# A quarter of the weights' low parts on another engine in one layer's first pass

## The chip, the core and the metric

The kernel runs on one core of a Trainium2 chip. Its engines work side by side and meet at semaphores: TensorE (PE) multiplies matrices, VectorE (DVE) and ScalarE (ACT) work element by element, GpSimd (POOL) does a few small things here, and SyncE's queue (SP) issues the loads. The metric is the device time of one execution in microseconds.

## What is computed

A trunk of two layers over 256 positions of width 2048. The first layer mixes with pooling and gated linear attention, the second with RWKV-7 and dilated attention; each has a feed-forward of width 8192 and a gate behind it. The second layer's mixer, cut to what matters:

```python
z = h @ w_in                                   # 2048 -> 6432
hc, hd = z[..., :RWKV_IN], z[..., RWKV_IN:]
c_out = rwkv7_time_mix(hc, mu, ...)            # r, k, v and three low-rank inputs from hc
q, k, v = jnp.split(hd, 3, axis=-1)            # dilated attention, with rotary q and k
...
mix = jnp.concatenate([c_out, d_out], axis=-1)
return mix @ w_out
```

All of it is in float32.

## The kernel before

Every large product is made of float32r products: a weight block of 128x1024 numbers is loaded as `raw`, ACT rounds it to `hi` (L257), and DVE makes the low part `lo = raw - hi` (L258). The activations are split likewise into `th` halves. PE adds three products, high by high, high by low and low by high; in `aform_run`, which serves the K, R and V projections, these are the matmuls of L353, L354 and L355, eight contraction tiles to a weight block, and L355 is the one that reads `lo`. In `bform_run` (L328 to L330) L329 reads it.

A weight block goes through `load` (SP's queue, five `raw` buffers), `parts_of` (ACT, then DVE; four buffers each of `hi` and `lo`) and PE. `take` keeps up to two blocks split and up to four in all ahead of the matmuls. In the RWKV layer `self.early` is 30, by which these instructions are given precedence over others.

A planner (Tile) sets the order of DVE's, ACT's, POOL's and SP's instructions by the order in which the program issues them and their precedence, and each engine then works its queue in order. PE's order is written by hand: in `odd`, a `Drive` runs streams (the projections) and chains (small work with due times, in microseconds of its own clock) and emits PE's instructions in that sequence.

In `odd` a first `drive.run` handles the low-rank inputs (six loads of L0, one of them made ahead by `lead`), then 24 blocks of K, R and V in this order, two loads each. The low-rank loads and the first two K loads are queued as four, one, two, one. Beside them run the chains `rate` (with POOL's copy into `decay`, L955), `norm` (squares `sq`, split into `sqh` and `sql`, and the matmul of L968), `operands` and `inner` (the matmuls of L1028). This run ends when the last of the eight `inner` is done, while V's projections still go on. Then new pools are opened, and POOL clears their tiles: EB, LB and CD (L1100), Z and XS (L1103, L1104). A second `drive.run` lets the rest of V, the attention's values and its rotary keys and queries stream on, and beside them `invert()`: transposes into `G` (L1142), 31 steps of a product and a sum on DVE (L821, L1149), and transposes back (L1151, L1153), whose result the matmuls of L1188 read. It ends when `invert()` and `begin()` are through. POOL has no other work of size in the layer.

Of the kernel before, what the change touches and what calls it, by code (L numbers as in the profile page):

```python
# [9 lines left out]
F32 = mybir.dt.float32  # L10
# [3 lines left out]
ALU = mybir.AluOpType  # L14
# [86 lines left out]
class Drive:  # L101
# [4 lines left out]
    def __init__(self):  # L106
        self.t, self.chains, self.streams = 0.0, [], []
# [44 lines left out]
class Trunk:  # L152
    def __init__(self, ctx, tc, a, out, parts=None, taps=None):
        self.tc, self.nc, self.a, self.out = tc, tc.nc, a, out
        self.parts, self.taps = parts, taps or {}
        pool = lambda name, bufs, **kw: ctx.enter_context(tc.tile_pool(name=name, bufs=bufs, **kw))
        self.const = pool("const", 1)
        self.keep = pool("keep", 1)
        self.wr, self.wh, self.wl = pool("wr", 5), pool("wh", 4), pool("wl", 4)
        self.tp = pool("tp", 18)  # L160
        self.acc = pool("acc", 3, space=PSUM)
        self.mp = pool("mp", 5, space=PSUM)
        self.small = pool("small", 3)

        self.gap = pool("gap", 1)
        self.junk = pool("junk", 2)
        self.rbp = pool("rbp", 1)
        nc = self.nc

        self.vec = self.const.tile([P, NVEC + 24], F32, name="vec")[:, :NVEC]  # L170
        nc.sync.dma_start(out=self.vec, in_=a["vec"])
        self.ident = self.const.tile([P, P], F32, name="ident")
        nc.sync.dma_start(out=self.ident, in_=self.cst("ident"))
        self.one = self.const.tile([P, P], F32, name="one")
        nc.vector.memset(self.one, 1.0)

        ps = self.mp.tile([P, 512], F32, name="mp")
        for n in range(10):
            nc.tensor.matmul(ps[:, :P], self.one, self.one, start=True, stop=True)
        self.eps = self.const.tile([P, 2], F32, name="eps")  # L180
        nc.vector.memset(self.gap.tile([P, 16], F32, name="gap"), 0.0)
        nc.vector.memset(self.eps[:, 0:1], EPS)
        nc.vector.memset(self.eps[:, 1:2], LN_EPS)
        self.x = [[self.keep.tile([P, 512], F32, name=f"x{tt}{c}") for c in range(4)] for tt in range(2)]
        self.ls = None
        self.early = 0
        self.pending, self.fetched, self.loaded, self.led = [], [], [], 0
        self.load_x(0)
        if parts and parts[0] != "even":
            for c in range(1, 4):  # L190
                self.load_x(c)
# [59 lines left out]
    def parts_of(self, raw, w, n):  # L251

        nc = self.nc
        hi = self.wh.tile([P, 1024], F32R, name="hi")
        lo = self.wl.tile([P, 1024], F32R, name="lo")
        with self.tc.high_priority(offset=self.early):
            nc.scalar.copy(out=hi[:, :w], in_=raw[:, :w])  # L257
            nc.vector.tensor_tensor(out=lo[:, :w], in0=raw[:, :w], in1=hi[:, :w].bitcast(F32), op=ALU.subtract)  # L258
        return (hi[:, :w].rearrange("p (a n) -> p a n", n=n), lo[:, :w].rearrange("p (a n) -> p a n", n=n))

    def split(self, ps, hi, lo, scale=None):
# [531 lines left out]
    def odd(self):  # L793
# [4 lines left out]
        nc, tc, a = self.nc, self.tc, self.a  # L798
        R0, K0, V0, L0, Q0 = 0, 1024, 2048, 3072, 3360
        w = a["od_w_in"]  # L800
# [22 lines left out]
        with ExitStack() as st:  # L823
# [76 lines left out]
            with ExitStack() as sa:  # L900
# [158 lines left out]
                def first():  # L1059
# [9 lines left out]
                    drive.chain(low(), W["low"], after_low)  # L1069
                    yield from kg  # L1070

                ll, kl = self.b_loads(w, L0, 288), self.a_loads(w, K0)
                self.queue(ll[:4] + kl[:1] + ll[4:] + kl[1:])
                drive.stream(first(), lambda: drive.chain(norm(0), W["key"], normed))
# [321 lines left out]
            def begin():  # L1396
                for g in begun:
                    for step in g:
                        if step[1] < 0:
                            break  # L1400
                        yield step
# [5 lines left out]
            drive.chain(invert(), W["inv0"], lambda: inverted.append(0))  # L1407
            drive.chain(begin(), W["begin"], lambda: inverted.append(1))
            drive.run(lambda: len(inverted) == 2)
            sb.__exit__(None, None, None)  # L1410

            drive.chain(gate_weights())
# [116 lines left out]
```

## Time and profile before

| | us |
|---|---|
| median of 3 runs | 2496.87 (2495.05 to 2496.88) |
| the profiled execution | 2495.14 |
| its span, first to last instruction | 2493.3 |
| busy PE / DVE / ACT / POOL | 2471.3 / 1544.2 / 1317.4 / 14.5 |
| `lo` on DVE (L258), 838 instructions | 1007.3, mean 1.21 each |

Busy times are sums over the span; an engine's idle time costs only where PE waits for it. The first pass of RWKV lies at about 1190 to 1392 us of the span. In a timeline a row is: start, duration, engine, line, operation, output and inputs, shape, count, and in brackets the idle time ahead of it with what ended it.

### The profile page before, as it was taken

Reading aid. Unit: us, or ns where it says so; the run is one execution under the profiler, and the core shown is the slowest. Engines: PE = TensorE matmul, PEld = TensorE weight load, DVE = VectorE, ACT = ScalarE, POOL = GpSimd, SP = SyncE. Lnnn points to the kernel's source line nnn. Section 1 sums busy time; section 2 is a strip of 40 time slices with the busy share of each in tenths; the row PEclk is TensorE's granted clock in tenths of the full one; section 3 lists DMA queues with packets and bytes.
Section 4 is the critical chain, followed back from the end, with each engine's and each line's share of the span. In section 5 each row is a group of like instructions: output and inputs, shape, how many; then the busy total and the mean of one; then the engine's idle time right before and its main releaser. Section 6 shows DMA issues by size and latency. Waiting matters only on the chain.

```text
span 2493.3 us, 36360 instructions
## 1 busy us (share of the span) xinstructions
PE 2471.3 (99%) x14202; PEld 2155.8 (86%) x14202; DVE 1544.2 (62%) x2121; ACT 1317.4 (53%) x1968; POOL 14.5 (1%) x32
## 2 busy tenths in 40 slices
PE   9999999999999999999999999999999999999999
PEld 8888988888888888888999999878888888888888
DVE  6665656555555555576689887656555555555574
ACT  7555546554444444465784565556454444444463
POOL 0000000000000000000000000000000000000000
PEclk9999999999999999999999999999999999999999
DMA  7635765666666666556768754656666666666654
GB/s 247 184 110 151 227 199 168 190 192 190 194 191 189 193 192 187 196 180 201 199 213 241 218 147 135 228 178 182 191 192 189 193 192 190 192 191 190 194 186 143
DMA packets 533084, 471.55 MB, mean 189 GB/s; under 512 B 40352, under 2 KB 417952, under 8 KB 532400
## 3 DMA queue, kind: packets, MB, share of 16 engines
q1 hardware_dynamic: 532912, 469.23, 62.2%
q8 instruction: 111, 1.82, 0.3%
q14 instruction: 61, 0.50, 0.1%
HBM read 456.57 MB, written 12.58 MB: 188 GB/s over the span
## 4 chain that ended last, share of the span: by engine, by line
PE 94%; DVE 3%; ACT 2%; issue 1%; DMA 1%; SPq 0%; DVEq 0%; ACTq 0%
PE acc L373 21%; PE acc L328 18%; PE acc L329 18%; PE acc L330 18%; PE acc L376 11%; PE acc L355 1%; PE acc L354 1%; PE acc L353 1%; DVE lo L258 1%; PE mp L721 1%; ACT hi L257 1%; PE mp L402 1%; DVE x L450 0%; PE mp L672 0%; PE mp L1028 0%
## 5 line engine op out<-in xcount | busy, mean ns | idle before, releaser
L258 DVE TENSOR_TENSOR lo<-raw,hi 128x1024 fp32r<-128x1024 f32 (+2 forms) x838 | 1007.3, 1210 | 768.7 <-ACT hi L257 523.0
L257 ACT CAST hi<-raw 128x1024 fp32r<-128x1024 f32 (+2 forms) x838 | 874.3, 1044 | 935.9 <-PE acc L330 588.2
L373 PE MATMUL acc<-th,hi 128*128 128x512 f32 x2240 | 538.1, 391 | 0.0
L373 PEld LDWEIGHTS acc<-th,hi 128*128 128x128 f32 x2240 | 412.0, 188 | 80.0
L328 PE MATMUL acc<-hi,th 128*128 128x512 f32 (+4 forms) x1248 | 439.1, 353 | 2.5 <-ACT th L264 1.2
L329 PE MATMUL acc<-lo,th 128*128 128x512 f32 (+4 forms) x1248 | 430.2, 345 | 0.4 <-DVE lo L258 0.4
L330 PE MATMUL acc<-hi,th 128*128 128x512 f32 (+4 forms) x1248 | 430.3, 346 | 0.0
L329 PE MATMUL acc<-lo,hh 128*128 128x512 f32 x1024 | 398.7, 389 | 0.0
L330 PE MATMUL acc<-hi,hl 128*128 128x512 f32 x1024 | 398.4, 389 | 0.0
L328 PE MATMUL acc<-hi,hh 128*128 128x512 f32 x1024 | 397.6, 391 | 0.0
L376 PEld LDWEIGHTS acc<-th,lo 128*128 128x128 f32 x2240 | 287.1, 191 | 10.8
L376 PE MATMUL acc<-th,lo 128*128 128x256 f32 x2240 | 290.9, 283 | 0.0
L328 PEld LDWEIGHTS acc<-hi,th 128*128 128x128 f32 x1248 | 235.6, 189 | 31.6 <-DVE y L1454 2.0
L330 PEld LDWEIGHTS acc<-hi,th 128*128 128x128 f32 x1248 | 235.5, 189 | 25.6 <-issue 0.3
L329 PEld LDWEIGHTS acc<-lo,th 128*128 128x128 f32 x1248 | 235.9, 189 | 24.7 <-DVE lo L258 0.7
L328 PEld LDWEIGHTS acc<-hi,hh 128*128 128x128 f32 x1024 | 192.2, 188 | 43.1 <-DVE h L382 3.5
L330 PEld LDWEIGHTS acc<-hi,hl 128*128 128x128 f32 x1024 | 192.2, 188 | 40.0
L329 PEld LDWEIGHTS acc<-lo,hh 128*128 128x128 f32 x1024 | 192.3, 188 | 38.6
L355 PE MATMUL acc<-th,lo 128*128 128x256 f32 x384 | 108.9, 284 | 2.7 <-DVE lo L258 2.7
L353 PE MATMUL acc<-th,hi 128*128 128x256 f32 x384 | 109.3, 285 | 0.0
L354 PE MATMUL acc<-th,hi 128*128 128x256 f32 x384 | 108.6, 283 | 0.0
L486 DVE TENSOR_TENSOR hl<-h,hh 128x512 fp32r<-128x512 f32 x64 | 44.2, 691 | 82.6 <-ACT hh L485 82.6
(319 smaller groups left out, 1754.6 us busy)
## 6 DMA issues: line engine op xcount, KB each, us to landing
raw<-in_ffn_up_dram SPq DMA_DIRECT2D x256, 512.0 KB, 4.0
raw<-in_ffn_down_dram SPq DMA_DIRECT2D x256, 512.0 KB, 4.2
raw<-in_od_w_in_dram SPq DMA_DIRECT2D x96, 512.0 KB, 4.3
raw<-in_ple_gate_dram SPq DMA_DIRECT2D x64, 512.0 KB, 4.4
raw<-in_ev_w_in_dram SPq DMA_DIRECT2D x56, 512.0 KB, 4.3
raw<-in_ev_w_out_dram SPq DMA_DIRECT2D x32, 512.0 KB, 4.3
raw<-in_od_w_out_dram SPq DMA_DIRECT2D x32, 512.0 KB, 4.1
raw<-in_ev_w_in_dram SPq DMA_DIRECT2D x24, 384.0 KB, 3.5
```

What stands on the lines that cost most here:

```text
L257: nc.scalar.copy(out=hi[:, :w], in_=raw[:, :w])
L258: nc.vector.tensor_tensor(out=lo[:, :w], in0=raw[:, :w], in1=hi[:, :w].bitcast(F32), op=ALU.subtract)
L328: nc.tensor.matmul(ps[tt][:, :n], xh[:, t], wh[:, j], start=first and not (joint and tt), stop=False)
L329: nc.tensor.matmul(ps[tt][:, :n], xh[:, t], wl[:, j], start=False, stop=False)
L330: nc.tensor.matmul(ps[tt][:, :n], xl[:, t], wh[:, j], start=False, stop=last and not (joint and not tt))
L353: nc.tensor.matmul(ps, wh[:, j], xh, start=k + j == 0, stop=False)
L354: nc.tensor.matmul(ps, wh[:, j], xl, start=False, stop=False)
L355: nc.tensor.matmul(ps, wl[:, j], xh, start=False, stop=k + j == kts - 1)
L373: nc.tensor.matmul(ps[e], ws[e][0][:, j], xT[k + j].both, start=k + j == 0, stop=False)
L376: nc.tensor.matmul(ps[e][:, :S], ws[e][1][:, j], xT[k + j][0], start=False, stop=k + j == kts - 1)
L402: nc.tensor.transpose(ps[:, tt * P:(tt + 1) * P], self.x[tt][k // 4][:, (k % 4) * P:(k % 4 + 1) * P], self.ident)
L486: nc.vector.tensor_tensor(out=lo, in0=h2, in1=hi.bitcast(F32), op=ALU.subtract)
```

## The change

A counter `shared` is added to the trunk, and a switch `share`, which is set to 1 at the beginning of the first pass (behind the one low-rank part made ahead) and back to 0 when the second `drive.run` ends. While it is on, `parts_of` counts its calls, and for every fourth of them the subtraction `raw - hi` goes to POOL instead of DVE. The operands, buffers and precedence stay as they are.

```diff
+        self.share = self.shared = 0
...
             nc.scalar.copy(out=hi[:, :w], in_=raw[:, :w])
-            nc.vector.tensor_tensor(out=lo[:, :w], in0=raw[:, :w], in1=hi[:, :w].bitcast(F32), op=ALU.subtract)
+            self.shared += self.share
+            (nc.gpsimd if self.share and self.shared % 4 == 0 else nc.vector).tensor_tensor(
+                out=lo[:, :w], in0=raw[:, :w], in1=hi[:, :w].bitcast(F32), op=ALU.subtract)
...
+                self.share = 1
                 ll, kl = self.b_loads(w, L0, 288), self.a_loads(w, K0)
...
             drive.run(lambda: len(inverted) == 2)
+            self.share = 0
```

## Rows read from the trace of the kernel before

**Rows 1.** The page's first part: busy us, share of the span, instructions.

```profile
PE 2471.3 (99%) x14202; PEld 2155.8 (86%) x14202; DVE 1544.2 (62%) x2121; ACT 1317.4 (53%) x1968; POOL 14.5 (1%) x32
```

**Rows 2.** Table by stretch: length; busy PE, PEld, DVE, ACT, POOL; clock, DMA share, GB/s.

```profile
1196.00:1270.00 74.00, 71.71 (x588) 70.27 (x586) 51.55 (x77) 60.22 (x121) 4.20 (x7) 1.00 0.68 188
1270.00:1330.00 60.00, 58.65 (x494) 58.27 (x495) 56.54 (x118) 45.09 (x84) 0.25 (x1) 1.00 0.82 264
1330.00:1392.00 62.00, 59.28 (x490) 58.67 (x489) 60.27 (x109) 27.65 (x44) 4.53 (x13) 1.00 0.82 213
```

**Rows 3.** Waits of PE, 1190 to 1392 us: sum, times, longest.

```profile
PE acc L355 <- DVE lo L258: 2.7, 3, 1.1
PE mp L1028 <- ACT bd L1008: 1.3, 2, 1.0
```

**Rows 4.** Timeline of PE: start, duration, instruction, idle time ahead of it.

```profile
1361.17 0.39 PE L355 MATMUL acc<-th,lo 128*128 128x256 f32 x1 [1.15 <-DVE lo L258]
...
1364.95 0.39 PE L355 MATMUL acc<-th,lo 128*128 128x256 f32 x1 [0.64 <-DVE lo L258]
...
1369.03 0.39 PE L355 MATMUL acc<-th,lo 128*128 128x256 f32 x1 [0.93 <-DVE lo L258]
```

**Rows 5.** Timeline of DVE and PE: one low part (a12) and its first use.

```profile
1234.82 1.23 DVE L258 TENSOR_TENSOR lo<-raw,hi 128x1024 fp32r<-128x1024 f32 x1 [1.72 <-ACT hi L257]
...
1242.84 0.28 PE L355 MATMUL acc<-th,lo 128*128 128x256 f32 x1
```

**Rows 6.** Line L258, 1196 to 1330 us: duration min/median/max in ns, first and last start.

```profile
L258 DVE TENSOR_TENSOR lo<-raw,hi x38: 449/1224/1226, 1195.7 to 1327.4; 128x1024 fp32r<-128x1024 f32 x37, 128x288 fp32r<-128x288 f32 x1
```

**Rows 7.** Timeline of POOL: memsets.

```profile
1191.31 1.85 POOL L919 MEMSET bd<- 128x1024 f32 x2
...
1335.05 0.99 POOL L1100 MEMSET EB<- 128x512 f32 x2 [61.62 <-DMA rwkv_grams<-gram]
...
1338.49 0.20 POOL L1104 MEMSET XS<- 64x128 f32 x1
```

**Rows 8.** Timelines of POOL and DVE: two of the eight copies into decay.

```profile
1225.62 0.93 POOL L955 COPY decay<-e 128x4 f32<-128x4 f32 x1 [5.31 <-ACT e L952]
1233.21 0.19 POOL L955 COPY decay<-e 128x4 f32<-128x4 f32 x1 [6.66 <-ACT e L952]
...
1225.27 1.22 DVE L258 TENSOR_TENSOR lo<-raw,hi 128x1024 fp32r<-128x1024 f32 x1 [0.32 <-ACT hi L257]
```

**Rows 9.** Timelines of DVE, ACT and PE, 1330 to 1365 us.

```profile
1330.76 4.08 DVE L1142 STREAM_TRANSPOSE G<-L_all 32x1024 f32<-32x1024 f32 x2
1334.87 1.23 DVE L258 TENSOR_TENSOR lo<-raw,hi 128x1024 fp32r<-128x1024 f32 x1
...
1341.12 1.23 DVE L258 TENSOR_TENSOR lo<-raw,hi 128x1024 fp32r<-128x1024 f32 x1
...
1359.90 1.22 DVE L258 TENSOR_TENSOR lo<-raw,hi 128x1024 fp32r<-128x1024 f32 x1
...
1363.68 1.22 DVE L258 TENSOR_TENSOR lo<-raw,hi 128x1024 fp32r<-128x1024 f32 x1
...
1362.23 1.98 ACT L257 CAST hi<-raw 128x1024 fp32r<-128x1024 f32 x2
...
1339.71 0.28 PE L355 MATMUL acc<-th,lo 128*128 128x256 f32 x1
```

**Rows 10.** Timelines of DVE and PE: `sql` behind the low part of a10.

```profile
1228.41 1.23 DVE L258 TENSOR_TENSOR lo<-raw,hi 128x1024 fp32r<-128x1024 f32 x1 [1.52 <-ACT hi L257]
1229.55 0.42 DVE L265 TENSOR_TENSOR sql<-sq,sqh 128x256 fp32r<-128x256 f32 x1
...
1230.65 0.28 PE L968 MATMUL mp<-sql,pick 128*32 128x256 f32 x1
```

**Rows 11.** Tile L_all: duration min/median/max in ns, first and last start.

```profile
L1188 PE MATMUL mp<-L_all,LB x128: 196/196/217, 1407.9 to 1534.8; 128*32 128x32 f32 x128
...
L1153 DVE STREAM_TRANSPOSE L_all<-Dn x1: 2092/2092/2092, 1388.6 to 1388.6; 128x1024 f32<-128x1024 f32 x1
```

## The prediction

> **What bounds the kernel now.** I read the page first. PE is busy 99% of the span and DVE 62% [rows 1], so over the whole PE bounds it. [...] The waits of PE say it: over the whole region the low parts `lo` cost PE 2.7 us in three waits [rows 3]. In order of time these are 1.15, 0.64 and 0.93 us, all between 1360 and 1369 us [rows 4]. The next largest sum, 1.3 us, is a wait on ACT's copies `bd` [rows 3].
>
> So a faster DVE can return 2.72 us through `lo`. Everywhere else `lo` is early: for example, a part finished at 1234.82 + 1.23 = 1236.05 us is first used at 1242.84, 6.8 us later [rows 5]. Outside the inversion the change buys nothing by itself.
>
> **How many move, and which.** I call the half blocks of the K, R and V projections a0 to a47 (24 blocks, two loads each). One low-rank part is made ahead of the switch; the counter then runs over three more low-rank parts, a0, two low-rank parts, a1, a2 and so on. Its fourth is a0, its eighth a2, and from there every fourth: a2, a6, ... a46, thirteen with a0. The next are the third part of each four of the attention's value and rotary blocks (b2, b6, perhaps b10) until the inversion's chain is through: 15 or 16 in all. In the trace the 37 full parts up to 1327.4 us are a1 to a37 [rows 6], so the `lo` at 1334.87 is a38, and the three late ones are a45, a46, a47. Of the moved ones a38, a42 and a46 lie before or in the late stretch.
>
> **What DVE is spared.** Next to other DVE work a `lo` takes 1.14 us of DVE's time (1228.41 to the next start at 1229.55) [rows 10], so 16 of them are 18.2 us, of which three, 3.4 us, lie ahead of the last late wait.
>
> **What POOL takes for one.** No row shows POOL with two inputs. The low bound is its memset of the same 128x1024, which writes and reads nothing: 1.85 us for two, 0.93 each [rows 7]. The high bound is that the two reads and the write pass one after the other at that rate, 3 x 0.93, plus the 0.19 us that a copy of four columns takes [rows 8]: 3.0 us. I take 2.1 us, two reads after each other (1.86) plus 0.19, writes beside them. [...]
>
> **What it does to DVE meanwhile.** The eight small POOL copies of `decay` are the nearest rows. Four meet a `lo` that DVE has begun, and last 0.86 to 0.93 us; the other four last 0.19 to 0.25. The one at 1225.62 ends at 1226.55, and DVE's `lo` of 1225.27 ended at 1226.49; the one at 1233.21 meets no `lo` and takes 0.19 [rows 8]. So POOL's read of SBUF stands still while DVE reads two inputs from SBUF, and goes in as soon as DVE's instruction is through. Whether POOL in turn holds DVE no row shows: the cost to DVE lies between nothing and the full 2.1 us. I take the full hold for DVE instructions with both inputs in SBUF, because the one direction that the rows show is an exclusion and not a sharing. In the inversion nearly every DVE instruction is of that kind; the transposes, with one input, are not. [...]
>
> **The sum.** A moved part spares DVE 1.14 us and holds it 2.1: +0.96 us where DVE has no idle time.
>
> Up to 1330 us: the three waits on `lo` are the only ones of the region [rows 3], and the part shown was 6.8 us early [rows 5], so a microsecond or two more is hidden. One small result is close: `sql` runs behind a10's `lo`, and PE wants it at 1230.65 [rows 10]. POOL would hold from 1228.42 to 1230.5, `sql` would end at 1230.9, PE loses 0.3 us.
>
> a38: POOL's queue is in order, and the clearing of the new tiles (EB to XS) was issued ahead of it: DVE's own order has a38 behind the transposes `G` (1330.76) [rows 9], which are issued later than those memsets. They begin at 1335.05, held by a DMA, and end at 1338.69 [rows 7]. a38 ends at 1340.8; PE wants it at 1339.71 [rows 9] and so is 1.1 us late. DVE gains 1.14, but a39 (1341.12 now) waits for POOL until 1340.8: 0.3 earlier, in time. Were a38 ahead of the memsets it would run under the transposes and cost nothing.
> a42: +0.96, so a45's `lo` (1359.90 [rows 9]) comes 0.65 later. PE's delay against no waiting at all is then 1.15 + 0.65 = 1.8 us, 1.1 of it spent at a38.
> a46: its high part, the first of two from 1362.23 on [rows 9], follows 0.65 later and ends near 1363.9; POOL gets in behind the running instruction, near 1364.2, and ends at 1366.3, where DVE ended at 1364.90 [rows 9]. PE's delay: 1.79 + 1.4 = 3.2.
> a47: DVE is 0.65 + 0.96 = 1.6 later: 2.72 + 1.6 = 4.3 against 2.72 now.
>
> So +1.6 here, +0.3 above: +1.9 us. With a38 ahead of the memsets the same steps give +0.8 in place of +1.6. Beyond 1392 us I cost it at nothing: the inversion's last transpose ends at 1390.7, and the first matmul on its result starts at 1407.9 [rows 11], 17 us later; that cover would have to be gone first. A raw buffer comes free when its `lo` is done, and SP's queue stands behind a load that waits for one; there are five, and neither large wait of PE is on a load [rows 3], so I cost that at nothing too. Without that cover it would be a38's lateness once more, 1.1 us.
>
> The profiled execution took 2495.14 us with a span of 2493.3, so it would take 2497.0. The median of the runs shown, 2496.87, lies 1.7 above it, and so I forecast 2498.8.
>
> **The rivals.**
> 1. POOL's instruction is longer, and the loss shows. Place: a38 to a47. At 3.0 us the same steps give PE 2.0 late at a38, DVE 0.6 later at a39 and 2.5 at a45, 4.4 at a47, and 1.2 at `sql`: +5.6 us, 2502.5. It decides from about 2.9 us on. For it: the high bound is 3.0, and more waiting behind DVE's instructions would come on top. Against: 2.1 lies nearer to the memset.
> 2. POOL and DVE don't hold each other in the other direction. Then DVE is three parts ahead by a47 (3.4 us), the three waits go, and only a38's 1.1 may be new: -1.6 to -2.7 us, 2494.2 to 2495.3. For it: no row shows DVE held. Against: rows 8.
> 3. The planner sets another order. It orders each queue itself, PE's excepted, so sixteen instructions moved may shift others on DVE, ACT and SP. For it: many DVE instructions around the inversion are ready at once. Against: the parts are issued with the same lead as before. PE's idle time in the three stretches, 2.29 + 1.35 + 2.72 = 6.4 us [rows 2], gives the scale either way: 2490.5 to 2503.3.
>
> **How the numbers follow.** A measurement of this kernel can tell about 0.2%, 5 us, from no change: 2491.9 to 2501.9. Forecast, held DVE with POOL at 1.9 to 2.9 us: 0.60, within. Rival 2: 0.15, within. Rival 1: 0.15, slower. Rival 3: 0.10, of it 0.04 faster, 0.02 within, 0.04 slower. So faster 0.04, same 0.77, slower 0.19. The range runs from rival 2 on the lowest run (2495.05 - 2.7 = 2492.4) to rival 1 on the highest, a little beyond 3.0 us: 2503.0.
>
> **What would show it.** POOL: 15 or 16 TENSOR_TENSOR of about 2.1 us, longer by up to 1.2 where a `lo` of DVE runs. DVE: instructions with two SBUF inputs stretched, or idle, by up to 2 us beside each, and PSUM-fed ones and transposes not. PE: a new wait on a POOL `lo` near 1340, one at a46 of about 1.4 us, a sum of 4 to 5 us on `lo` in place of 2.7. It is wrong if DVE's two-input instructions beside POOL keep their 0.42 and 1.22 us, if POOL takes under 1.5 or over 2.9 us, or if PE's waits change mostly outside 1330 to 1392 us.

## The result and the profile after

The changed kernel took 2514.28 us (median of 4 runs, 2512.17 to 2515.35) against 2496.88 us before: 1.0071 times as long, 95% interval 1.0059 to 1.0082, or 17.4 us more. That is slower, and well outside the forecast's range of 2492.4 to 2503.0 us. The profiled execution took 2513.97 us with a span of 2512.2.

The page's first part, as in [rows 1]:

```profile
PE 2479.8 (99%) x14202; PEld 2162.4 (86%) x14202; DVE 1546.8 (62%) x2105; ACT 1316.8 (52%) x1968; POOL 54.2 (2%) x48
```

DVE has 16 instructions fewer and is busy 2.6 us longer (an instruction that is held counts as busy, 2.35 us in place of 0.16 in the third pair below): what it was spared came back. POOL has the 16 instructions forecast. Line L261 over 1170 to 1400 us, where 14 of them lie (duration min/median/max in ns, first and last start):

```profile
L261 POOL TENSOR_TENSOR lo<-raw,hi x14: 2373/2404/3142, 1195.0 to 1388.0; 128x1024 fp32r<-128x1024 f32 x14
```

The table by stretch, over nearly the work of [rows 2]: length; busy PE, PEld, DVE, ACT, POOL; granted clock, DMA share, GB/s.

```profile
1198.00:1272.00 74.00, 69.86 (x562) 68.25 (x561) 47.17 (x66) 57.04 (x117) 16.52 (x12) 0.98 0.65 180
1272.00:1337.00 65.00, 60.98 (x508) 59.85 (x508) 60.18 (x114) 46.89 (x85) 9.73 (x5) 1.00 0.72 229
1337.00:1411.00 74.00, 66.30 (x519) 65.16 (x518) 66.19 (x110) 31.17 (x50) 18.41 (x19) 0.95 0.75 201
```

PE is idle 4.1, 4.0 and 7.7 us (length less busy) where it was idle 2.29, 1.35 and 2.72. New is the clock column: 0.98 and 0.95 in two stretches where it was 1.00. The seven largest waits of PE over 1190 to 1425 us, as in [rows 3] (sum, times, longest):

```profile
PE acc L359 <- DVE lo L261: 6.9, 3, 2.5
PE mp L972 <- DVE sql L269: 2.3, 4, 1.1
PE mp L1032 <- DVE op L825: 1.9, 2, 1.4
PE mp L934 <- ACT zl L1059: 1.8, 2, 1.3
PE mp L994 <- DVE invl L269: 1.2, 1, 1.2
PE mp L1329 <- DVE ro L1320: 1.2, 1, 1.2
PE acc L359 <- POOL lo L261: 0.8, 1, 0.8
```

The low parts `lo` cost 7.7 us in place of 2.7, as the forecast's kind of loss but larger; and about as much again is lost on small results that the forecast hardly looked at. The largest one by one, as in [rows 4]: the second operand block, then a39, a45, a46 and a47.

```profile
1312.20 0.35 PE L1032 MATMUL mp<-op,bd 128*128 128x128 f32 x1 [1.45 <-DVE op L825]
...
1353.67 0.39 PE L359 MATMUL acc<-th,lo 128*128 128x256 f32 x1 [2.48 <-DVE lo L261]
...
1375.28 0.58 PE L359 MATMUL acc<-th,lo 128*128 128x256 f32 x1 [2.43 <-DVE lo L261]
...
1380.61 0.39 PE L359 MATMUL acc<-th,lo 128*128 128x256 f32 x1 [0.76 <-POOL lo L261]
...
1385.78 0.39 PE L359 MATMUL acc<-th,lo 128*128 128x256 f32 x1 [2.02 <-DVE lo L261]
```

**DVE is held, and to the end of POOL's instruction.** Three pairs from the timelines of POOL and DVE, POOL's subtraction first:

```profile
1232.70 2.40 POOL L261 TENSOR_TENSOR lo<-raw,hi 128x1024 fp32r<-128x1024 f32 x1 [1.91 <-ACT hi L259]
1232.96 2.43 DVE L269 TENSOR_TENSOR sql<-sq,sqh 128x256 fp32r<-128x256 f32 x1 [1.82 <-ACT sqh L268]
...
1309.40 2.37 POOL L261 TENSOR_TENSOR lo<-raw,hi 128x1024 fp32r<-128x1024 f32 x1 [15.62 <-ACT hi L259]
1309.53 2.52 DVE L825 TENSOR_TENSOR op<-r,e 128x256 f32<-128x256 f32 x1
...
1327.28 2.38 POOL L261 TENSOR_TENSOR lo<-raw,hi 128x1024 fp32r<-128x1024 f32 x1 [15.51 <-DMA raw<-in_od_w_in_dram]
1327.34 2.35 DVE L1004 TENSOR_SCALAR op<-op 128x4 f32<-128x4 f32 x1
```

The last of these DVE instructions in the kernel before:

```profile
1318.31 0.16 DVE L1000 TENSOR_SCALAR op<-op 128x4 f32<-128x4 f32 x1
```

`sql` took 0.42 us in [rows 10]; here it ends at 1235.39, 0.28 us behind POOL. The second pair is what makes PE wait 1.45 us at 1312.20. The third was not foreseen: a scaling of four columns, with one SBUF input, was held as well, and took 2.35 us in place of 0.16. The pair at 1232.70 also shows that DVE's load is beside the point there: DVE had been idle for 1.82 us before `sql`, and the hold cost what it cost.

**Half clock behind PE's waits.** PE's granted clock around the two longest waits (table by stretch):

```profile
1350.00:1354.00 4.00, 1.52 (x12) 1.32 (x12) 3.97 (x6) 3.88 (x8) 0.00 (x0) 1.00 0.60 101
1354.00:1358.00 4.00, 4.00 (x24) 4.00 (x23) 3.93 (x11) 1.58 (x3) 0.01 (x1) 0.59 0.84 193
1358.00:1362.00 4.00, 4.00 (x35) 4.00 (x35) 3.90 (x6) 0.84 (x1) 2.54 (x1) 0.99 1.00 259
...
1375.00:1379.00 4.00, 3.72 (x19) 3.72 (x20) 3.86 (x10) 2.39 (x3) 1.09 (x1) 0.57 0.48 133
```

Behind the wait that ends at 1353.67 PE works without a pause and gets through 24 matmuls in 4 us where 35 pass in the next 4. The record of the granted clock has it at 0.50 of its full value for 3.41 us from 1354.69, from 1375.17, and from 1211.33, behind two waits of 1.27 and 0.56 us on `zl`: each costs about 1.7 us, by an estimate (half of 3.41). Before, the pass had none.

**The account.** From a0's first `lo` matmul to a38's, and from there to the last rotary block's (b23): length, PE's idle time in it (gaps over 0.06 us), time at half clock. The kernel before has 141.25 and 122.55 us, of which idle 3.64 and 3.60, and no half clock. All are worked out from the traces, the runs below among them; the last column is the difference of the medians.

| kernel | first half | idle | half clock | second half | idle | half clock | whole time |
|---|---|---|---|---|---|---|---|
| changed | +6.7 | +4.5 | 3.4 | +10.4 | +6.5 | 6.8 | +17.4 |
| extra_read | +12.7 | +8.8 | 6.8 | +10.7 | +8.2 | 3.4 | +25.0 |
| extra_write | -0.1 | -0.1 | 0 | +0.1 | +0.1 | 0 | +1.5 |
| no_read | +1.1 | +1.1 | 0 | +3.5 | +2.1 | 3.4 | +3.1 |
| first_run | +6.7 | +4.4 | 3.4 | +3.6 | +2.0 | 3.4 | +11.1 |
| second_run | +0.3 | +0.3 | 0 | +6.3 | +4.0 | 3.4 | +6.9 |
| eighth | +1.8 | +1.3 | 0 | +5.2 | +4.5 | 0 | +7.2 |
| extra_copy | +0.4 | +0.3 | 0 | +1.9 | +0.4 | 3.4 | +3.4 |
| under_transposes | +0.6 | +0.6 | 0 | -0.7 | -0.6 | 0 | -0.5 |
| early_60 | +0.4 | +0.4 | 0 | -1.0 | -0.9 | 0 | -0.7 |
| late_one | -0.2 | -0.2 | 0 | +0.7 | -0.2 | 3.4 | +1.5 |
| late_two | -0.4 | -0.2 | 0 | +2.0 | +1.2 | 3.4 | +3.2 |
| transposes_60 | -0.5 | -0.3 | 0 | +0.2 | +0.3 | 0 | -0.2 |

Idle time and half the time at half clock make up the lengths to within 1 us in every row: for the changed kernel 4.5 + 1.7 = 6.2 of 6.7 and 6.5 + 3.4 = 9.9 of 10.4 us. The 1.8 us that remain of the span's 18.8 are another stretch at half clock at 37 us, ahead of anything the change touches; such stretches in the first 45 us come and go in the profiles of the other kernels too (start +2.1 us with extra_write, +4.4 with eighth), so it is not put down to the change.

### The profile page after: what moved, and what is told of

Read it like the earlier page. It is cut to its first block, busy times and chain, and to the rows that moved or that the text cites. A ratio compares the mean times of both kernels' runs of the same rounds, so it can differ in the third digit from the quotient of the medians.

```text
span 2512.2 us, 36349 instructions
## 1 busy us (share of the span) xinstructions
PE 2479.8 (99%) x14202; PEld 2162.4 (86%) x14202; DVE 1546.8 (62%) x2105; ACT 1316.8 (52%) x1968; POOL 54.2 (2%) x48
## 3 DMA queue, kind: packets, MB, share of 16 engines
q8 instruction: 111, 1.82, 0.3%
## 4 chain that ended last, share of the span: by engine, by line
PE 91%; DVE 4%; ACT 2%; DMA 1%; issue 1%; SPq 0%; DVEq 0%; ACTq 0%
PE acc L377 20%; PE acc L332 18%; PE acc L334 17%; PE acc L333 17%; PE acc L380 11%; DVE lo L261 1%; ACT hi L259 1%; PE mp L725 1%; PE acc L359 1%; PE acc L357 1%; PE acc L358 1%; PE mp L406 1%; DVE x L454 0%; DMA rwkv_grams<-gram 0%; PE mp L676 0%
## 5 line engine op out<-in xcount | busy, mean ns | idle before, releaser
L261 DVE TENSOR_TENSOR lo<-raw,hi 128x1024 fp32r<-128x1024 f32 (+3 forms) x822 | 989.0, 1212 | 769.1 <-ACT hi L259 523.9
```

Source lines behind the costliest of these rows:

```text
L261: (nc.gpsimd if self.share and self.shared % 4 == 0 else nc.vector).tensor_tensor(out=lo[:, :w], in0=raw[:, :w], in1=hi[:, :w].bitcast(F32 ...
```

## The experiments

Theory H says that POOL's reads of SBUF hold DVE and that this is the loss; theory P that it is the planner's new order, since DVE's queue differs in 144 lines (16 of them the parts that left it).

**POOL subtracts, but in addition.** DVE keeps all its parts.

```diff
             nc.vector.tensor_tensor(out=lo[:, :w], in0=raw[:, :w], in1=hi[:, :w].bitcast(F32), op=ALU.subtract)
+            self.shared += self.share
+            if self.share and self.shared % 4 == 0:
+                nc.gpsimd.tensor_tensor(out=self.spare[:, :w], in0=raw[:, :w], in1=hi[:, :w].bitcast(F32),
+                                        op=ALU.subtract)
```

> The kernel before with one thing added: DVE keeps every low part, and for every fourth part of the first pass POOL makes the same subtraction once more, into a tile that nobody reads. DVE's queue keeps the order of before but for some two dozen instructions (the changed kernel has 144 in other places). Theory H (DVE is held while POOL reads SBUF): nothing is spared and 16 holds of 2.4 us remain, so at least the loss of the changed kernel (+17 us) and up to 16 x 1.14 = 18 us more: 2512 to 2532 us. Theory P (the loss comes from the planner's new order of DVE's, ACT's and SP's queues): 2495 to 2501 us.

2520.81 us, 1.0100 (1.0086 to 1.0113). DVE's order is nearly that of before, and the loss is larger than the changed kernel's: theory P falls as the main cause. A low part on DVE beside one on POOL, POOL first:

```profile
1382.42 2.65 POOL L263 TENSOR_TENSOR spare<-raw,hi 128x1024 f32<-128x1024 f32 x1 [17.32 <-ACT hi L259]
...
1382.76 3.39 DVE L260 TENSOR_TENSOR lo<-raw,hi 128x1024 fp32r<-128x1024 f32 x1
```

DVE's 1.22 us have become 3.39, ending 1.08 us behind POOL, which is about the time that the part takes by itself: it stood still for POOL's whole instruction. Ten of POOL's sixteen subtractions last 3.2 to 4.7 us here in place of 2.4, since both engines now work on the same parts, so this loss is not that of the changed kernel's holds alone.

**POOL as busy, but only writing.**

```diff
+            if self.share and self.shared % 4 == 0:
+                for m in (w, w, w // 2):
+                    nc.gpsimd.memset(self.spare[:, :m], 0.0)
```

> The kernel before with POOL clearing a tile that nobody reads, two and a half times 128x1024 (some 2.3 us by the 0.93 us of a memset), at the same sixteen places where the other kernel subtracts; DVE keeps every low part. POOL is as busy as in the changed kernel and reads nothing. Theory H (POOL's read is what holds DVE): 2495 to 2499 us, no DVE instruction stretched. Theory P (order): the same. A third theory W (any POOL instruction beside DVE's holds it, a write too): as with the extra subtraction, 2512 us or more.

2497.29 us, 1.0005 (0.9996 to 1.0014): no difference. The lines by form over 1190 to 1400 us (times | busy us, mean ns | idle before):

```profile
L264 POOL MEMSET spare<- 128x1024 f32 x32 | 30.6, 957 | 56.7 <-PE mp L1035 55.1
L264 POOL MEMSET spare<- 128x512 f32 x16 | 8.4, 527 | 0.9
```

POOL works 39 us on these, as long as on its 16 subtractions, and no low part of DVE takes over 1.3 us (1.22 in the mean, as before). So what held the low part of 3.39 us above was POOL's read, not POOL's being busy. A scaling with one SBUF input was held by a write alone. In no_read, the next experiment, where POOL only clears:

```profile
1284.77 0.95 POOL L262 MEMSET lo<- 128x1024 f32 x1 [9.54 <-PE acc L361]
1284.80 0.94 DVE L1006 TENSOR_SCALAR op<-op 128x4 f32<-128x4 f32 x1
```

That is 0.94 us in place of 0.16, to the end of the memset. In extra_write some scalings are stretched in this way, the longest, of 128x128, to 0.70 us in place of 0.29, but no wait of PE on them shows.

**DVE spared, nothing read.** The low parts that POOL would make are set to zero, so their share of the products is left out.

```diff
-            (nc.gpsimd if self.share and self.shared % 4 == 0 else nc.vector).tensor_tensor(...)
+            if self.share and self.shared % 4 == 0:
+                nc.gpsimd.memset(lo[:, :w].bitcast(F32), 0.0)
+            else:
+                nc.vector.tensor_tensor(out=lo[:, :w], in0=raw[:, :w], in1=hi[:, :w].bitcast(F32), op=ALU.subtract)
```

> The changed kernel with POOL's sixteen subtractions replaced by a memset of the low part to zero, so that this part's product of the activations with the weights' low parts is left out: DVE is spared the same sixteen instructions, POOL reads nothing, and DVE's queue has the order of the changed kernel but for six lines. Theory H: the hold is gone and the spared 16 x 1.14 us remain; the waits on low parts at the inversion's end (2.7 us) go: 2492 to 2498 us. Theory P: the order is that of the changed kernel and so is most of its loss: 2506 to 2513 us.

2498.88 us, 1.0011 (1.0002 to 1.0019). In nearly the changed kernel's order (six lines of DVE's queue differ), without the read, all but 3.1 of its 17.4 us are gone: H. But the gain that H expected isn't there either; the time is 3.1 us over before (0.5 to 4.7 by the interval). Its waits of PE on low parts:

```profile
PE acc L361 <- DVE lo L264: 4.4, 2, 2.4
```

DVE was spared 18 us, and the waits on the last parts are 1.7 us longer than in [rows 3]. The likely reason is that the planner put the time to other work: with a38 gone from DVE's queue, its order sets three of the four transposes `G` in a row and the inversion's steps ahead of the late parts.

**The two halves.** The switch goes off at the end of the first run (ten parts moved), or works only in the second (six, the count as in the changed kernel).

```diff
                 drive.run(lambda: done["ops"] == 8 and not drive.chains)
+                self.share = 0
```

> The changed kernel with the switch off from the end of the first run on: POOL makes ten parts (a0, a2 and every fourth up to a34), DVE all of the matrix inversion's. The first hold theory, by which the loss lies where DVE's results are late for PE in the inversion alone (my forecast: +0.3 us ahead of it): 2496 to 2498 us. The theory now, that small results of DVE ahead of it (the squares' low parts, operands, z) are late too: +6 to +9 us by the shift of the changed kernel's a36 (6.7 us ahead of before's, less the first 40 us), 2502 to 2505 us.

2507.12 us, 1.0046 (1.0032 to 1.0060): +11.1 us, more than either expectation. The first half of the pass gives the +6.7 us expected of the theory now. The rest comes in the second half, where POOL has no part at all: its transposes `G` start later against PE (how, stands further below).

> The changed kernel with the switch on only in the second run, the count as in the changed kernel: POOL makes six parts (a38, a42, a46, b2, b6, b10). My forecast had +1.6 us for these: 2497 to 2499 us. The theory now, that here DVE's late low parts and the stretches at half clock behind PE's waits cost 8 to 10 us: 2504 to 2507 us. If the two halves add up, this one's loss and that of the first run come to 17 us; well under that sum would mean that late results of the first run make the second worse.

2502.88 us, 1.0028 (1.0017 to 1.0040): +6.9 us. The two add up to 18.0 against 17.4, alike within what these measurements tell (each interval is some 3 us to either side): no sign that the one makes the other worse. The moved part itself is among the late ones here: PE waits 2.2 us for a POOL `lo`.

**Half as many.** Every eighth part in place of every fourth (`% 8`).

> The changed kernel with every eighth part on POOL in place of every fourth: a2, a10, a18, a26, a34, a42 and two later ones, eight in place of sixteen. If each hold costs by itself, where it falls: about half the loss, 2503 to 2506 us. If the loss comes from DVE's load in all (a moved part holds 2.4 us and spares 1.14, so that DVE gets later and later): less than half, since DVE catches up between them, 2497 to 2501 us.

2503.14 us, 1.0029 (1.0018 to 1.0041): +7.2 us, 0.41 of the loss for half the holds. That is at the low end of the first expectation and above the second: the loss doesn't come from DVE's load in all. It is no even price per hold either: the first half loses 1.8 us in place of 6.7, the second 5.2 in place of 10.4, and in the pass no stretch at half clock comes with it.

**A copy in place of the subtraction,** again in addition.

```diff
+                nc.gpsimd.tensor_copy(out=self.spare[:, :w], in_=raw[:, :w])
```

> The kernel before with POOL copying the raw block of every fourth part into a tile that nobody reads (one input in place of two); DVE keeps every low part, and its queue has the order of before but for eight lines. Theory H1 (any read of SBUF by POOL holds DVE, for as long as it reads): about half of the extra subtraction's loss of 25 us, 2504 to 2512 us, with DVE's instructions stretched to the end of POOL's copy. Theory H2 (only a POOL instruction with two inputs holds it): 2495 to 2499 us.

2499.39 us, 1.0013 (1.0005 to 1.0022): +3.4 us, between the two expectations. The hold is there; POOL's copy first:

```profile
1287.19 1.28 POOL L263 COPY spare<-raw 128x1024 f32<-128x1024 f32 x1 [11.41 <-DMA raw<-in_od_w_in_dram]
...
1287.49 2.06 DVE L260 TENSOR_TENSOR lo<-raw,hi 128x1024 fp32r<-128x1024 f32 x1
```

So H1 holds in its mechanism (2.06 us in place of 1.22) and not in its price. A copy lasts 1.04 us where it meets nothing (1.33 in the mean of the sixteen), less than half of 2.39, and costs less than a seventh (3.4 of 25 us): it seems that the slack covers a hold of 1 us nearly everywhere, and one of 2.4 us in many places not.

**One part, under the transposes.** POOL makes a38 alone, with the clearing of the tiles behind it.

```diff
-            (nc.gpsimd if self.share and self.shared % 4 == 0 else nc.vector).tensor_tensor(
+            (nc.gpsimd if self.share and self.shared in (44,) else nc.vector).tensor_tensor(
...
+            with tc.high_priority(offset=-60):
                 for t in EB + LB + CD:
                     nc.gpsimd.memset(t, 0.0)
...
+            with tc.high_priority(offset=-60):
                 for n in range(2):
                     clear(n)
```

> POOL makes one low part alone, a38, and the clearing of the inversion's tiles stands behind it in POOL's queue, so that the subtraction runs beside DVE's transposes, which the trace of the changed kernel shows at their usual time. Theory H: no hold that counts, DVE is spared 1.14 us ahead of the three late parts: 2494.5 to 2496.5 us, 0 to 2 us below before. Theory P (the planner puts what is spared to other work): 2496 to 2499 us, with the waits on the late parts as in before or longer.

```profile
1332.92 2.40 POOL L261 TENSOR_TENSOR lo<-raw,hi 128x1024 fp32r<-128x1024 f32 x1 [59.23 <-ACT hi L259]
...
1331.60 4.13 DVE L1149 STREAM_TRANSPOSE G<-L_all 32x1024 f32<-32x1024 f32 x2
```

2495.50 us, 0.9997 (0.9988 to 1.0006): no difference. Two transposes take 4.13 us beside POOL's 2.40, as against 4.08 alone [rows 9]: neither held the other. The waits on the late parts fall from 2.7 to 2.4 us only. Raising the lead from 30 to 60 in the second run, with nothing on POOL:

> The kernel before with the lead of the loads and of the two halves raised from 30 to 60 in the second run (nothing on POOL): an attempt to bring the three late parts of the inversion forward on DVE, where the inversion's own steps have 17 us of cover. If the planner follows: the 2.7 us of waits go, 2493 to 2495 us. If it doesn't: 2495 to 2499 us.

2495.24 us, 0.9997 (0.9988 to 1.0006): no difference. Two waits on low parts are left, of 0.78 and 1.19 us. And both together:

> The two edits that left the time of before within its measurement, together: one low part on POOL beside DVE's transposes, and the lead raised to 60 in the second run. If their gains of 0.7 and 1.0 us in the second half of the pass add up: 2494 to 2495 us, 1 to 2 us below before, at the edge of what a measurement tells. If the planner gives the spared time to the inversion's steps again: 2495 to 2498 us, no difference.

2496.72 us, 1.0001 (0.9992 to 1.0010): no difference. No version found beats the kernel before.

**Is the half clock PE's wait's doing?** In the kernel before, a45's low part is made twice or three times.

```diff
+            for _ in range(2 if self.shared == 51 else 1):
```

> The kernel before with one DVE instruction more: the low part of a45 is made twice, so that PE waits at it for 1.2 us more than the 1.15 us of before (about 2.4 us). No part is on POOL. Theory C (a wait of PE of this length in this dense stretch is followed by 3.41 us at half clock, 1.7 us more): +2.9 us, 2498.9 us, and the granted clock at 0.5 right behind the wait. Theory N (the stretches at half clock come by themselves): +1.2 us, 2497.2 us, the clock at 1.0.

> The same with a45's low part made three times: PE waits 2.4 us more than in before, about 3.6 us. Theory C: +4.1 us, 2500.1 us, and the granted clock at 0.5 right behind the wait. Theory N: +2.4 us, 2498.4 us.

2497.53 us, 1.0005 (0.9997 to 1.0014), and 2499.23 us, 1.0013 (1.0004 to 1.0022). PE's wait in late_one, and the stretches around it:

```profile
1362.47 0.58 PE L359 MATMUL acc<-th,lo 128*128 128x256 f32 x1 [2.62 <-DVE lo L262]
...
1356.00:1362.00 6.00, 3.84 (x33) 3.64 (x31) 5.76 (x13) 2.14 (x3) 0.00 (x0) 1.00 0.65 209
1362.00:1366.00 4.00, 3.53 (x17) 3.53 (x18) 3.90 (x9) 1.44 (x2) 0.00 (x0) 0.57 0.53 141
1366.00:1372.00 6.00, 6.00 (x53) 6.00 (x52) 5.93 (x11) 3.35 (x4) 0.00 (x0) 1.00 0.56 169
```

The clock falls at this wait in both kernels, with nothing on POOL: 0.03 us before its end in late_one, 0.54 us before it in late_two, whose wait is 4.09 us. That is theory C. The totals of both theories were too high, because PE, once late, finds a46 and a47 ready, and the two waits of [rows 4] (0.64 and 0.93 us) go. Without them theory N comes to -0.1 and +1.4 us and theory C to +1.6 and +3.1; the medians are +1.5 and +3.2. An interval is some 2 us to either side, so the clock in the traces says more than the times. But a wait doesn't always bring the half clock: the profile of eighth has one of 2.37 us, and that of extra_read one of 2.97, ended at 1359.33, with the clock at 1.00. The stretch of extra_read:

```profile
1354.00:1362.00 8.00, 5.03 (x42) 4.82 (x41) 7.94 (x12) 4.41 (x10) 0.49 (x2) 1.00 0.94 200
```

What decides between the two, these runs don't tell.

## Why the prediction was wrong

**Right: the mechanism.** Sixteen parts were moved, those named. The full hold, chosen against rival 2, is what the traces show: DVE's short instructions with two SBUF inputs ended 0.2 to 0.3 us behind POOL's (`sql` of 2.43 us 0.28 behind), and PSUM-fed ones (`gram`, 0.69 us beside a38, 0.68 before) and transposes (4.13 us for two in under_transposes, 4.08 before) kept their time. POOL's writes alone cost no time that can be told (extra_write, +1.5 us). The prediction left the scalings out: that of four columns took 2.35 us beside the subtraction and 0.94 beside a memset, in place of 0.16.

**Nearly right: POOL's 2.1 us.** It is 2.37 to 2.41 where nothing is ahead of it. A part holds 2.4 and spares 1.14: +1.26 and not +0.96. By the prediction's own steps that makes +3.1 us in place of +1.9, far from +17.4.

**Wrong: "up to 1330 us ... a microsecond or two more is hidden", +0.3.** This step failed most. The one place that the prediction worked out, `sql` behind a10, came at its size (0.38 us against 0.3). But [rows 5] shows the slack of a `lo`, and from it the step took the slack of DVE. The `lo` did stay early: a12's ends at 1240.81 and is used at 1247.66, as far ahead as before. What DVE does in or behind a held instruction is used at once: `sql` (0.38 and 0.47 us of PE, a10 and a18), `invl` behind a `lo` stretched to 1.52 us (1.20, before 0.26) and `op` twice (1.45 and 0.46). With the loads of the next paragraph the first half lost 6.7 us, and first_run shows that its ten parts cost 11.1 in all. The sign of it was there before the change: the list of PE's waits goes on, below the two lines of [rows 3], with small results of DVE that PE already waited for, and that had no slack at all:

```profile
PE mp L968 <- DVE sql L265: 0.7, 1, 0.7
...
PE mp L990 <- DVE invl L265: 0.3, 1, 0.3
```

**Wrong: raw buffers and SP's queue, "nothing".** a0's `lo` stood in POOL's queue behind memsets and ended at 1197.37; on DVE it ended at 1193.18 (the whole pass starts 1.8 us later in this profile). SP's queue stands behind loads that wait for such buffers: one goes out at 1198.65, when a low-rank part on DVE is done (1198.62; 1194.79 before), and the low-rank weight, issued at 1196.22 before, at 1201.68, when a1's is (1201.65). ACT's queue has its rounding ahead of `zl`:

```profile
1201.68 1.20 SPq L897 DMA_DIRECT2D raw<-in_rwkv_w_dram  x2
...
1206.63 1.05 ACT L898 CAST w<-raw 128x1024 fp32r<-128x1024 f32 x1 [2.62 <-DMA raw<-in_rwkv_w_dram]
...
1208.80 1.88 ACT L1059 ACTIVATE zl<-acc,rstd 128x256 f32<-128x256 f32 x6
```

`zl` began at 1204.88 before. PE waits 1.27 and 0.56 us for it, and the stretch at half clock behind them makes it 3.5 us, for a step priced at nothing or, without cover, at 1.1. In eighth, where a0 stays on DVE, the weight is issued as long after the pass's start as before, and PE doesn't wait for `zl`. In extra_read the load is as late (1200.75) with a0 on DVE, but ACT has `zl` ahead of the rounding and PE doesn't wait: POOL's work on a0 and the planner's order act together here.

**Wrong in place and size: 1330 to 1392 us, +1.6.** a38 was not late: the planner put it ahead of the memsets, and it was done at 1342.93, five microseconds early.

```profile
1340.52 2.41 POOL L261 TENSOR_TENSOR lo<-raw,hi 128x1024 fp32r<-128x1024 f32 x1 [10.86 <-ACT hi L259]
1346.32 0.99 POOL L1105 MEMSET EB<- 128x512 f32 x2 [3.40 <-DMA rwkv_grams<-gram]
```

The loss began with a39 instead. The transposes start late, and three stand in a row:

```profile
1341.09 1.29 DVE L1035 TENSOR_TENSOR gram<-mp,mask_g 128x512 f32<-128x512 f32 x2 [1.75 <-DMA rwkv_grams<-gram]
...
1343.39 6.12 DVE L1147 STREAM_TRANSPOSE G<-L_all 32x1024 f32<-32x1024 f32 x3
...
1352.40 1.22 DVE L261 TENSOR_TENSOR lo<-raw,hi 128x1024 fp32r<-128x1024 f32 x1
```

Before, they began 8.95 us ahead of PE's use of a38's low part (1330.76 and 1339.71 [rows 9]); now 4.76 us ahead (1343.39, 1348.15). In first_run the lead is 5.36 us and PE waits 3.01 us for a39, with no part of the second half on POOL in that run; in no_read it is 7.45 and there is no such wait. So the first run delays the inversion, and the inversion delays a39. The row of `gram` shows how: DVE sits idle for 1.75 us until a transfer has read the one tile that its last `gram` products go into. That transfer was issued late, at 1336.37, because DVE made the products ahead of it late: behind the last operand block, which a34's hold (the third pair above) had pushed back. Hold and order both take part: extra_read, with the hold and nearly the order of before, has a wait of 1.46 us and a lead of 5.36; no_read, with nearly this order and no hold at that place, 0.68 and 7.45; before has no wait at this place. Three transposes in a row do not do it alone: second_run has them too, at the old lead of 8.95, and PE doesn't wait for a39. At a45 to a47 the waits are 2.43, 0.76 and 2.02 us, 5.2 in all, where the steps gave a delay of 4.3 in all, 1.1 of it spent at a38.

**Missing: the clock.** The sum had PE's waits at their length. Three stretches at half clock in the pass, of 3.41 us each, add 5.1 us by the estimate above, of 17.1. In [rows 2], where no wait was longer than 1.15 us, the granted clock was 1.00, and nothing there showed this price.

**Beyond 1392, nothing:** nearly so. The cover held (transposes done at 1403.1, first use at 1426.3, as [rows 11]); a new wait of 1.15 us on `ro` at 1419.61 comes in, and one of 0.61 at the first matmul of `XS` shrinks to 0.29.

**The rivals.** Rival 1 had the sign, by a POOL instruction of 2.9 us or more, and that isn't the cause: it took 2.4. Rival 2 fell with the hold; and no_read, where POOL's part is also shorter (0.95 us), shows +3.1 us without it and not -1.6 to -2.7, it seems because the planner spends the time elsewhere. Rival 3, the planner, did set another order; alone it is worth about those 3 us.

**The signs of being wrong.** None of the three that the prediction set came up clearly: the two-input instructions were held, POOL took 2.4 us where nothing was ahead of it, and of PE's new idle time 6.5 us lie behind a38's first use and 4.5 ahead of it. They watched the mechanism; the slack of the small results, the step that failed, had no sign of its own but the place of the waits.

## What to carry to other kernels

Before moving an operation with SBUF inputs to POOL, list what DVE would run beside it and when each result is wanted, the small ones in a chain first: a hold of 2.4 us costs where the next result has less slack than that, however idle DVE is: `sql` cost PE 0.38 us behind 1.82 us of idle DVE. Slack read from one kind of result says nothing of another. And where PE runs without pause, price a new wait above its length: here two of the changed kernel's three waits of over 2 us (2.48 and 2.43, not the one of 2.02) brought a stretch of 3.41 us at half clock with them, about 1.7 us more each by an estimate.

## What was not expected of the hardware

- A scaling on DVE with one SBUF input (128x4) was held for POOL's whole subtraction, 2.35 us in place of 0.16, and such a scaling was held by a memset too, which reads nothing (0.94 us); a one-input copy by POOL held a two-input subtraction of DVE, 2.06 us in place of 1.22 beside a copy of 1.28.
- Around the end of waits of PE of 1.7 to 4.1 us (from 0.5 us before it to 1.5 behind), and behind two of 1.1 to 1.3 and 0.56 us close together, the granted clock went to 0.50 for 3.41 us, at about 1.7 us each by an estimate, in eight of the kernels' profiles; behind others of up to 2.97 us it stayed at 1.00.
